# All gate projections ahead of the merge, through DRAM, and a time reserve in the choice of TensorE's next matmul

## The chip, the cores and the metric

The kernel runs as one program on one core of a Trainium2 chip. The metric is the device time of an execution in microseconds (us). The profiled execution is a single one, with its own time; the comparison is made on the median of timed runs.

## What is computed

Two layers of a decoder trunk, over 576 tokens: 512 of a prompt and 64 of eight sampled sequences. One input projection feeds two branches, retention and sparse attention; each branch is gated by a SiLU and projected back to the model's width, and the two are merged by per-channel sigmoid gates:

```python
def decoder_layer(x, p_i, pos, ret_s0, past, topk, ...):
    h = rmsnorm(x, g_norm)
    rq, rk, rv, rz, aq, ak, av, az, iq, ik, iw, gr, ga = in_projection(h, w_in, pos, q_gain, k_gain)
    o_r, s_new = retention(rq, rk, rv, ret_s0)
    o_r = group_norm_heads(o_r).reshape(B, T, RET_HEADS * RET_DV).astype(x.dtype)
    u_r = jnp.einsum('bte,ed->btd', o_r * jax.nn.silu(rz), w_o_ret)
    o_a = sparse_attention(...)          # indexer, top-k, softmax over the chosen keys
    u_a = jnp.einsum('bte,ed->btd', o_a * jax.nn.silu(az), w_o_att)
    m = jax.nn.sigmoid(gr) * u_r + jax.nn.sigmoid(ga) * u_a
    x = x + jnp.einsum('btd,de->bte', m, w_out)
    gate = jax.nn.sigmoid(jnp.einsum('btd,de->bte', x, w_ple_gate))
    x = x + gate * jnp.einsum('btp,pd->btd', p_i, w_ple_proj)
```

The width is 1024, cut into KT = 8 blocks of 128 channels. The gates `gr` and `ga` are 1024 wide each, so each has eight blocks.

## The kernel before

Activations stand transposed, channels on the partitions and tokens along the row: a block is a tile of 128 x 576. Every fp32 operand is split into a high and a low part, and a product takes three matmuls (high x high, high x low, low x high). A **unit** is one weight tile of 128 x 1024: it is loaded by SP's queue into one of two staging buffers (`wst`), split by ACT (`whi`) and DVE (`wlo`), and used by `proj_a` in 48 matmuls of 288 columns (two halves of the tokens, eight blocks, three products). The results of a half stand in one of three PSUM banks named `pm` until DVE or ACT has taken them out.

The order of the instructions is made by a planner in the kernel itself. Each piece of work is a generator that yields operations. `Streams` keeps one modelled clock for each engine and, of all operations that are next in their generators, issues the one with the earliest start; ties go to the lower priority number and then to the older generator. The start is the later of the engine's clock and the time at which the operands are ready. `MARGIN` adds 0.15 us to that ready time for an operation on DVE and 0.1 us for one on ACT, when what it waits for is another engine's work. The result is a fixed order on each engine; the semaphores then make the hardware wait wherever the plan was too early.

The main generator of a layer goes through `PLAN`: the projections of keys (`kx`), indexer (`iq`), values (`rv`), SiLU gate (`az`), attention queries (`aq0`, `aq1`), four retention heads (`rq`, `rk`, `rz` each), then the gates of blocks 0 and 1, and then, for each block d, the output projections `wo` with the merge, followed by the gates of block d + 2. The attention, the indexer's top-k and the retention run as side generators with tiles of their own (`tq`, `ta`, `oT`, `tr`, `acc` are their PSUM banks, one each). The merge begins when all of them have ended (`for e in sides: yield e`). A gate's result is held from its projection to its merge in one of four 576-column slots (`ZS`) cut from the tile `misc`:

```python
                z = yield Get(ZS)
                zt[st] = z
```

The step of the merge multiplies the slot by the output projection, half by half (`mul`), adds the two slots and splits the sum (`fin`), and gives the slots back.

Of the kernel before, what the change touches and what calls it, by code (L numbers as in the profile page):

```python
# [99 lines left out]
    return a, rot  # L100


MARGIN = {"DVE": 0.15, "ACT": 0.1}


class Op:
# [89 lines left out]
class Streams:  # L196
# [15 lines left out]

    def spawn(self, gen, prio):
        self.count += 1
        self.run.append(([gen, prio, self.count, None, 0.0], None))

    def put(self, slots, item):
        if slots.queue:
# [11 lines left out]
    def _advance(self, st, value):  # L230
        gen = st[0]
        while True:
            try:
                x = gen.send(value)
            except StopIteration:
                return
            value = None
            if isinstance(x, Op):
                st[3] = x
                st[4] = self._ready(x)  # L240
                self.heads.append(st)
                return
            if isinstance(x, Get):
                if x.slots.free:
                    value = x.slots.free.pop(0)
                    continue
                x.slots.queue.append(st)
                return
            if x.n > 0:
                x.queue.append(st)  # L250
                return

    def _ready(self, op):
        t = 0.0
        for boxes, w in ((op.ins, False), (op.outs, True)):
            for name, p0, p1, c0, c1 in boxes:
                for e in self.log.get(name, ()):
                    if (w or e[6]) and e[0] < p1 and p0 < e[1] and e[2] < c1 and c0 < e[3]:
                        r = e[4] + self.HOP.get((e[5], op.eng), 0.15)
                        if e[5] != op.eng:  # L260
                            r += MARGIN.get(op.eng, 0.0) 
                        if r > t:
                            t = r
        return t

    def _note(self, op, end):
        low = min(self.clock["PE"], self.clock["DVE"], self.clock["ACT"]) - 5.0
# [11 lines left out]
    def go(self):  # L279
        clock = self.clock  # L280
        while True:
            while self.run:
                st, value = self.run.pop(0)
                self._advance(st, value)
            if not self.heads:
                return
            best = None
            for i, st in enumerate(self.heads):
                key = (max(clock[st[3].eng], st[4]), st[1], st[2])
                if best is None or key < best[0]:  # L290
                    best = (key, i)
            st = self.heads.pop(best[1])
            op = st[3]
            start = best[0][0]
            op.fn(*op.a, **op.k)  # L295
            if op.form != self.form and op.eng == "PE":
                start += 0.09
                self.form = op.form
            end = start + op.dur
            clock[op.eng] = end  # L300
            if op.eng == "SP" and op.name != "page":
                size = _val((op.a[0] if op.a else op.k["out"]).nbytes)
                self.dma = max(self.dma, start + 1.1) + size / 0.35e6
                end = self.dma + 1.0
            self._note(op, end)
            self._advance(st, None)
# [3 lines left out]
def tile_hybrid_decoder(ctx: ExitStack, tc: tile.TileContext, A, O):  # L310
# [46 lines left out]
    cosr, sinr = rot[:, 0:T], rot[:, T:2 * T]  # L357
    ssq = rot[:, 0:TX]
    xd = dp.tile([128, KT, T], FT, name="xd")
    WST = slots(cp, "wst", [128, 1024], FT, 2)  # L360
    WHI = slots(cp, "whi", [128, 1024], FR, NSLOT["hi"])
    WLO = slots(cp, "wlo", [128, 1024], FR, NSLOT["lo"])
# [199 lines left out]
    def layer(l, xh, xl, kxb):  # L562
# [693 lines left out]
        for st in PLAN:  # L1256
            name, i = st[0], st[1:]
            if name == "kx":
                for j in range(5):
                    K.spawn(kx(j, kxb[j]), 0)  # L1260
            elif name == "iq":
                yield from proj_b(U("iq"), 260, 3, xh, xl, (1, 4, 2, 3), iqx)
            elif name == "rv":
                yield from proj_b(U(*st), 256, 4, xh, xl, range(5), rvx(i[0]))
            elif name == "aq":
                yield from proj_b(U(*st), 256, 4, xh, xl, range(5), aqx(i[0]))
            elif name == "az":
                yield from proj_a(U(*st), 0, mv, KT, silu(silz[1][:, i[0]], e_az))
                drop(U(*st))
            elif name in ("rq", "rk", "rz"):  # L1270
                h = i[0]
                t = views(h)
                if name == "rz":
                    ev = silu(silz[0][:, h], e_h[h])
                else:
                    ev = ropeT(t["qT" if name == "rq" else "kT"], e_h[h], e_hd[h - 2] if h > 1 else None)
                yield from proj_a(U(*st), 0, mv, KT, ev)
                drop(U(*st))
                if name == "rz":
                    side(ret_p(h, t), PRIO["ret_p"])  # L1280
                    side(ret_s(h, t), PRIO["ret_s"])
            elif name in ("gr", "ga"):
                if name == "gr" and i[0] == 0:
                    for e in list(e_q.values()) + list(e_iq.values()) + [e_k, e_rr]:
                        yield e
                    ZS = zslots(0, 4)
                z = yield Get(ZS)
                zt[st] = z

                def gate(z):  # L1290
                    def evac(ps, cs):
                        yield V.tensor_tensor(z[:, cs], ps[:, :TH], R[:, cs], OP.mult)
                        K.put(BANK["pm"], ps)
                        yield S.activation(z[:, cs], z[:, cs], AF.Tanh, scale=0.5)

                    return evac

                yield from proj_a(U(*st), 0, mv, KT, gate(z))
                drop(U(*st))
            elif name == "wo":  # L1300
                continue
            elif name == "merge":
                d = i[0]
                if la is None:
                    for e in sides:
                        yield e
                    atc.__exit__(None, None, None)
                    yh = xp.tile([128, KT, TX], FR, name="xh")
                    yl = xp.tile([128, KT, T], FR, name="xl")
                    lac = tc.tile_pool(name="la", bufs=1, reuse_waits="tile")  # L1310
                    la = lac.__enter__()
                    oh = [la.tile([128, 4, T], FR, name=f"oh{x}") for x in range(2)]
                    ol = [la.tile([128, 4, T], FR, name=f"ol{x}") for x in range(2)]
                    e_o = [[Event() for _ in range(4)] for _ in range(2)]
                    for x in range(2):
                        for c in range(4):
                            K.spawn(then(split(oh[x][:, c], ol[x][:, c], silz[x][:, c]), e_o[x][c]), 0)
                    e_m = [Event() for _ in range(KT)]

                th = [zt["gr", d], zt["ga", d]]  # L1320

                def mul(z, ev):
                    def evac(ps, cs):
                        yield V.scalar_tensor_tensor(z[:, cs], z[:, cs], 1.0, ps[:, :TH], op0=OP.add, op1=OP.mult)
                        free(ps)
                        K.set(ev)

                    return evac

                def fin(d, th, ev):  # L1330
                    yield ev
                    yield V.tensor_tensor(th[0], th[0], th[1], OP.add)
                    K.put(ZS, th[1])
                    yield from split(yh[:, d, :T], yl[:, d], th[0])
                    K.put(ZS, th[0])
                    K.set(e_m[d])

                ev = Event(4)
                u = U("wo", d)
                for x in range(2):  # L1340
                    yield from proj_a(u, x * 512, (oh[x], ol[x]), 4, mul(th[x], ev), 0, None if d else e_o[x],
                                      ("oT", "acc") if x and not d else ("pm", "pm"))
                drop(u)
                K.spawn(fin(d, th, ev), 0)
# [159 lines left out]
def _plan(order):  # L1504
    p = []
    for t in order.split():
        n, i = t[:2], t[2:]
        p += [(n,)] if not i else [("rq", int(i)), ("rk", int(i)), ("rz", int(i))] if n == "rt" else [(n, int(i))]
    p += [("gr", 0), ("ga", 0), ("gr", 1), ("ga", 1)]
    for d in range(KT):  # L1510
        p += [("wo", d), ("merge", d)]
        p += [("gr", d + 2), ("ga", d + 2)] if d + 2 < KT else []
    return p + [("wout", d) for d in range(KT)] + [("pp", 0), ("pp", 1)] + [("wpg", d) for d in range(KT)]


# [86 lines left out]
```

## Time and profile before

| | |
|---|---|
| timed runs, median of 3 (lowest to highest) | 1151.29 us (1149.56 to 1151.41) |
| the profiled execution, its own time | 1149.36 us |
| its span, first to last instruction | 1147.4 us |
| mean granted TensorE clock | 0.989 of full speed |
| PE busy | 1099.3 us (96%) |
| DVE busy | 762.7 us (66%) |
| ACT busy | 525.9 us (46%) |
| DMA, mean | 92 GB/s |

All operations are recorded through one helper, so every row bears the line L295; the tiles' names tell the work apart. A matmul's row begins when it starts and lasts until its modelled end, which overlaps the next one: the distance of two starts is the rate. `pm<-xh,whi` is a matmul that writes a `pm` bank from the activations `xh` and the weights `whi`. An "idle before" in brackets is time in which the engine's last row had ended and the next had not begun.

### The profile page before, as it was taken

To read this page: it belongs to the slowest core of one execution; us is meant where nothing else is said; L and a number is where in the kernel's file an instruction comes from. 1 tells how busy PE (TensorE), PEld (TensorE's weight loads), DVE (VectorE), ACT (ScalarE), POOL (GpSimd) and SP (SyncE) were. 2 spreads that over 40 slices of the span, in tenths; PEclk is the share of its full clock that TensorE was granted. 3 is DMA by queue.
4 is the path that set the end of the run, shared out by engine and by line. 5 is a ranking of instruction groups with operands and counts; after the bars stand their busy time and mean duration, and the time that the engine had idled before them with its cause. 6 is when DMAs were issued, how large, how long until landed. Compare 5 with 4: busy or idle time off the path is not lost.

```text
span 1147.4 us, 21421 instructions
## 1 busy us (share of the span) xinstructions
PE 1099.3 (96%) x8426; PEld 1054.0 (92%) x8426; DVE 762.7 (66%) x1979; ACT 525.9 (46%) x1116; POOL 57.9 (5%) x68
## 2 busy tenths in 40 slices
PE   7999799999999999999999996999999999999998
PEld 7889688798899999999998996988899999999998
DVE  6899998667673535543659999886676644454433
ACT  6643455566652222234446434556676422223331
POOL 0100111000000000000010011100000000000000
PEclk9999989999999999999999998999999999999999
DMA  6532121231212222523335212113121222235231
GB/s 193 167 94 82 38 70 60 83 125 54 81 56 93 75 92 74 185 84 113 97 119 163 73 55 75 62 53 130 58 76 62 77 87 81 86 112 158 83 120 47
DMA packets 43894, 105.91 MB, mean 92 GB/s; under 512 B 6418, under 2 KB 18578, under 8 KB 43794
## 3 DMA queue, kind: packets, MB, share of 16 engines
q1 hardware_dynamic: 43794, 104.55, 28.1%
q8 instruction: 66, 1.08, 0.4%
q14 instruction: 34, 0.28, 0.1%
HBM read 93.61 MB, written 10.91 MB: 91 GB/s over the span
## 4 chain that ended last, share of the span: by engine, by line
PE 68%; DVE 23%; ACT 4%; issue 2%; DMA 2%; SPq 0%; POOL 0%; DVEq 0%; ACTq 0%; POOLq 0%
PE pm L295 56%; DVE xl L295 6%; DVE sm L295 5%; DVE wlo L295 3%; PE acc L295 3%; PE tq L295 3%; PE oT L295 3%; DVE misc L295 2%; PE tr L295 2%; PE ta L295 2%; DVE t2k L295 1%; DVE silz L295 1%; DVE qs L295 1%; ACT t2k L295 1%; ACT tb L295 1%
## 5 line engine op out<-in xcount | busy, mean ns | idle before, releaser
L295 PE MATMUL pm<-xh,whi 128*128 128x288 f32 x1536 | 460.0, 299 | 1.0 <-DVE misc L295 1.0
L295 PE MATMUL pm<-xh,wlo 128*128 128x288 f32 x1536 | 458.6, 299 | 0.0
L295 PE MATMUL pm<-xl,whi 128*128 128x288 f32 x1536 | 458.5, 299 | 0.0
L295 PEld LDWEIGHTS pm<-xh,whi 128*128 128x128 f32 x1536 | 292.1, 190 | 2.5 <-DVE misc L295 1.3
L295 PEld LDWEIGHTS pm<-xl,whi 128*128 128x128 f32 x1536 | 292.3, 190 | 1.4 <-issue 0.4
L295 PEld LDWEIGHTS pm<-xh,wlo 128*128 128x128 f32 x1536 | 291.8, 190 | 0.6
L295 ACT ACTIVATE whi<-wst 128x1024 fp32r<-128x1024 f32 (+4 forms) x148 | 150.3, 1017 | 241.2 <-PE pm L295 170.5
L295 DVE TENSOR_TENSOR wlo<-wst,whi 128x1024 fp32r<-128x1024 f32 (+4 forms) x148 | 173.0, 1171 | 85.9 <-ACT whi L295 85.9
L295 PE MATMUL pm<-whi,xh 128*128 128x256 f32 (+2 forms) x416 | 119.5, 293 | 5.5 <-DVE misc L295 2.7
L295 PE MATMUL pm<-wlo,xh 128*128 128x256 f32 (+2 forms) x416 | 119.1, 293 | 0.3 <-DVE wlo L295 0.2
L295 PE MATMUL pm<-whi,xl 128*128 128x256 f32 (+2 forms) x320 | 91.4, 286 | 0.0
L295 PEld LDWEIGHTS pm<-whi,xh 128*128 128x128 f32 x416 | 80.9, 194 | 7.2 <-DVE misc L295 3.4
L295 DVE TENSOR_TENSOR misc<-pm,R 128x288 f32<-128x288 f32 x64 | 29.2, 457 | 83.2 <-PE pm L295 81.7
L295 PEld LDWEIGHTS pm<-wlo,xh 128*128 128x128 f32 x416 | 80.8, 194 | 2.3 <-issue 1.2
L295 ACT ACTIVATE t2k<-t2k,sm 128x256 f32<-128x256 f32 (+3 forms) x111 | 62.5, 578 | 33.2 <-DVE sm L295 30.6
L295 PE MATMUL pm<-oh,whi 128*128 128x288 f32 x240 | 70.9, 296 | 0.0
L295 PE MATMUL pm<-oh,wlo 128*128 128x288 f32 x240 | 70.9, 296 | 0.0
L295 PE MATMUL pm<-ol,whi 128*128 128x288 f32 x240 | 70.9, 295 | 0.0
L295 PEld LDWEIGHTS pm<-whi,xl 128*128 128x128 f32 x320 | 60.5, 189 | 0.1
L295 DVE SCALAR_TENSOR_TENSOR misc<-misc,pm 128x288 f32<-128x288 f32 x60 | 26.8, 452 | 39.3 <-PE pm L295 39.3
L295 DVE MAX8 sm<-xl 128x8 f32<-128x512 f32 (+2 forms) x96 | 52.4, 549 | 0.5
L295 DVE MATCH_REPLACE8 xl<-sm,xl 128x256 f32<-128x256 f32 (+2 forms) x96 | 51.7, 540 | 0.1
(258 smaller groups left out, 1714.5 us busy)
## 6 DMA issues: line engine op xcount, KB each, us to landing
wst<-in_wa SPq DMA_DIRECT2D x96, 512.0 KB, 3.5
wst<-in_wb SPq DMA_DIRECT2D x16, 512.0 KB, 4.0
wst<-in_wo SPq DMA_DIRECT2D x16, 512.0 KB, 3.5
s<-in_ckv SPq DMA_DIRECT2D x32, 128.0 KB, 2.6
s<-in_s SPq DMA_DIRECT2D x8, 512.0 KB, 4.5
out_rss<-s SPq DMA_DIRECT2D x8, 512.0 KB, 2.7
x<-in_xT SPq DMA_DIRECT2D x8, 288.0 KB, 5.9
misc<-in_xT SPq DMA_DIRECT2D x8, 288.0 KB, 3.7
```

Of the source, the lines that this page charges most:

```text
L295: op.fn(*op.a, **op.k)
```

## The change

First, `PLAN` puts all sixteen gate projections of a layer ahead of the merge. Their results can't stay in four slots, so each is written to a DRAM tile (`zd`) when both halves have gone through the tanh, and the slot is given back (`spill`); when the main generator comes to the merge, `fetch` reads the blocks back in order, two slots each, as slots come free.

Second, the planner keeps two times for each operation: the ready time as modelled, and a safe one with the margin. It chooses by the safe one and sets the engine's clock by the modelled one. TensorE gets a margin, 1.0 us. For DVE and ACT the margins stay in the choice and no longer move the clock.

```diff
-MARGIN = {"DVE": 0.15, "ACT": 0.1}
+MARGIN = {"DVE": 0.15, "ACT": 0.1, "PE": 1.0}
...
                         r = e[4] + self.HOP.get((e[5], op.eng), 0.15)
-                        if e[5] != op.eng:
-                            r += MARGIN.get(op.eng, 0.0) 
                         if r > t:
                             t = r
-        return t
+                        if e[5] != op.eng:
+                            r += MARGIN.get(op.eng, 0.0)
+                        if r > safe:
+                            safe = r
+        return t, safe
...
-                key = (max(clock[st[3].eng], st[4]), st[1], st[2])
+                key = (max(clock[st[3].eng], st[5]), st[1], st[2])
...
-            start = best[0][0]
+            start = max(clock[op.eng], st[4])
...
+    zd = {(l, n, d): dp.tile([128, T], FT, name=f"z{n}{l}{d}") for l in range(DEPTH) for n in ("gr", "ga")
+          for d in range(KT)}
...
                 z = yield Get(ZS)
-                zt[st] = z
+                ev = Event(2)
...
+                def spill(z, ev, dst):
+                    yield ev
+                    yield SP.dma_start(dst, z)
+                    K.put(ZS, z)
+
+                K.spawn(spill(z, ev, zd[(l,) + st]), 0)
...
+                    e_g = {k: Event() for k in range(KT)}
+
+                    def fetch():
+                        for k in range(KT):
+                            for n in ("gr", "ga"):
+                                z = yield Get(ZS)
+                                yield SP.dma_start(z, zd[l, n, k])
+                                zt[n, k] = z
+                            K.set(e_g[k])
+
+                    K.spawn(fetch(), 0)
...
+                yield e_g[d]
                 th = [zt["gr", d], zt["ga", d]]
...
-    p += [("gr", 0), ("ga", 0), ("gr", 1), ("ga", 1)]
+    p += [(n, d) for d in range(KT) for n in ("gr", "ga")]
     for d in range(KT):
         p += [("wo", d), ("merge", d)]
-        p += [("gr", d + 2), ("ga", d + 2)] if d + 2 < KT else []
```

The change reorders all engines. Three places show it.

**TensorE, first layer, in the middle of the retention heads and the attention of the second query block.** `acc` and `tr` are banks of the retention, `ta` holds transposed softmax weights, `oT` their product with the values, `pm` a projection. Before:

```order
L295 MATMUL ta_72<-cst,xl 128x128 x2
L295 MATMUL tr_74<-cst,xh 128x128 x2
L295 MATMUL acc_75<-xh 128x128 x2
L295 MATMUL acc_75<-xh,xl 128x128
L295 MATMUL acc_75<-xh 128x128
L295 MATMUL acc_75<-xh,xl 128x128
L295 MATMUL oT_73<-pth_392,vhl 128x256
L295 MATMUL acc_75<-xh 128x128
L295 MATMUL tr_74<-iqs_386,iqs_387 128x512 x2
L295 MATMUL oT_73<-ptl_393,vhl 128x256
```

Now, at the same pair of transposes:

```order
L297 MATMUL ta_72<-cst,xl 128x128 x2
L297 MATMUL acc_75<-xh 128x128
L297 MATMUL ta_72<-cst,t2k_426 128x128 x2
L297 MATMUL pm_68<-xh,whi_123 128x288
L297 MATMUL pm_68<-xl,whi_123 128x288
L297 MATMUL pm_68<-xh,wlo_126 128x288
L297 MATMUL pm_68<-xh,whi_123 128x288
L297 MATMUL pm_68<-xl,whi_123 128x288
L297 MATMUL tr_74<-iqs_418,iqs_419 128x512 x2
L297 MATMUL pm_68<-xh,wlo_126 128x288
L297 MATMUL pm_70<-xh,whi_121 128x288
L297 MATMUL acc_75<-xh 128x128
```

Where side matmuls stood one behind the other, projection matmuls now stand between them.

**VectorE, first layer, where the second set of attention queries (`aq1`) begins.** `MAX` and `MATCH_REPLACE` are rounds of the indexer's top-k on score rows of 384 and 512 columns, `ptl` the low part of the softmax weights, `qs` the low part of the queries. Before:

```order
L295 TENSOR_TENSOR ptl_393<-ta_72,pth_392 128x256
L295 MATCH_REPLACE xl<-sm_384,xl 128x384
L295 MAX sm_382<-xl 128x8
L295 RECIPROCAL sm_380<-sm_380 128x1
L295 MAX sm_383<-xl 128x8
L295 MATCH_REPLACE xl<-sm_382,xl 128x512
L295 MATCH_REPLACE xl<-sm_383,xl 128x384
L295 MAX sm_385<-xl 128x8
```

Now:

```order
L297 TENSOR_TENSOR ptl_425<-ta_72,pth_424 128x256
L297 MAX sm_417<-xl 128x8
L297 MATCH_REPLACE xl<-sm_417,xl 128x384
L297 RECIPROCAL sm_416<-sm_416 128x1
L297 MAX sm_414<-xl 128x8
L297 MATCH_REPLACE xl<-sm_414,xl 128x384
L297 TENSOR_SCALAR xl<-xl 128x384
L297 SCALAR_TENSOR_TENSOR xl<-t2k_428,xl 128x512
```

Two top-k ran side by side here; now the one of 384 columns ends, and the scores of the one of 512 are only being summed.

**SP's queue, first layer, in the merge.** `in_wo` and `in_wa` are weight units, `zgr` and `zga` the gates' DRAM tiles. Before:

```order
L295 DMA wst_87<-in_wo 128x1024
L295 DMA wst_88<-in_wa 128x1024
L295 DMA wst_87<-in_wa 128x1024
L295 DMA wst_88<-in_wo 128x1024
L295 DMA wst_87<-in_wa 128x1024
```

Now:

```order
L297 DMA misc<-zgr_88 128x576
L297 DMA zga_102<-misc 128x576
L297 DMA wst_119<-in_wo 128x1024
L297 DMA misc<-zga_96 128x576
L297 DMA misc<-zgr_89 128x576
L297 DMA wst_120<-in_wo 128x1024
L297 DMA misc<-zga_97 128x576
L297 DMA misc<-zgr_90 128x576
```

Each weight unit of the merge now stands behind two reads of gates.

## Rows read from the trace of the kernel before

**Rows 1.** The page's first part: busy us, share of the span, instructions
```profile
PE 1099.3 (96%) x8426; PEld 1054.0 (92%) x8426; DVE 762.7 (66%) x1979; ACT 525.9 (46%) x1116; POOL 57.9 (5%) x68
```

**Rows 2.** Busy us by stretch: PE, PEld, DVE, ACT, POOL; then clock, DMA share, GB/s
```profile
0.00:50.00 50.00, 41.95 (x295) 40.39 (x295) 35.19 (x111) 34.65 (x81) 5.48 (x10) 1.00 0.55 172
50.00:125.00 75.00, 72.13 (x558) 68.02 (x557) 73.78 (x225) 30.84 (x66) 4.03 (x4) 1.00 0.29 91
125.00:160.00 35.00, 26.45 (x173) 24.41 (x172) 31.98 (x108) 15.02 (x35) 6.12 (x6) 0.85 0.19 59
160.00:330.00 170.00, 164.26 (x1337) 148.85 (x1336) 126.40 (x381) 106.11 (x258) 12.71 (x15) 0.99 0.23 77
330.00:600.00 270.00, 269.94 (x2030) 269.69 (x2029) 133.09 (x206) 98.29 (x166) 3.42 (x5) 1.00 0.32 103
...
675.00:715.00 40.00, 28.73 (x214) 26.72 (x212) 38.73 (x128) 17.72 (x40) 7.76 (x8) 0.94 0.19 56
715.00:910.00 195.00, 188.23 (x1497) 172.07 (x1498) 147.82 (x433) 117.89 (x279) 15.95 (x18) 0.99 0.22 75
```

**Rows 3.** PE's timeline: start, us, engine, operation, idle before; first in the merge
```profile
400.00 0.29 PE L295 MATMUL pm<-xh,wlo 128*128 128x288 f32 x1
400.13 0.29 PE L295 MATMUL pm<-xh,whi 128*128 128x288 f32 x1
...
46.34 0.28 PE L295 MATMUL pm<-whi,xl 128*128 128x256 f32 x1
47.77 0.55 PE L295 MATMUL ta<-cst,misc 128*128 128x128 f32 x3 [1.15 <-ACT misc L295]
```

**Rows 4.** PE's waits, 0 to 50 us: total us, times, longest
```profile
PE ta L295 <- ACT misc L295: 1.2, 1, 1.2
PE tr L295 <- POOL rcol L295: 0.9, 1, 0.9
```

**Rows 5.** PE's waits, 160 to 330 us
```profile
PE tr L295 <- DVE iqs L295: 1.4, 2, 0.8
...
PE tq L295 <- DVE sm L295: 1.0, 1, 1.0
```

**Rows 6.** PE's waits, 715 to 910 us
```profile
PE tr L295 <- DVE iqs L295: 1.9, 2, 1.5
```

**Rows 7.** PE's waits, 125 to 160 us
```profile
PE ta L295 <- DVE qs L295: 4.3, 3, 2.6
```

**Rows 8.** Timeline of all engines at one attention-query tile
```profile
136.53 0.44 PE L295 MATMUL ta<-cst,misc 128*128 128x128 f32 x2 [0.35 <-DVE qs L295]
...
138.34 0.42 DVE L295 TENSOR_TENSOR qs<-ta,qs 64x256 fp32r<-64x256 f32 x1
...
140.50 0.69 PE L295 MATMUL ta<-cst,misc 128*128 128x128 f32 x2 [2.58 <-DVE qs L295]
```

**Rows 9.** The five stretches at half clock, as Rows 2: the first, their sum
```profile
140.00:147.00 7.00, 4.89 (x20) 4.20 (x20) 6.74 (x20) 3.01 (x6) 1.57 (x2) 0.51 0.00 1
...
sum 24.00, PE 20.70 PEld 19.02 DVE 22.27 ACT 7.24 POOL 7.97; mean PE 4.14 PEld 3.80 DVE 4.45 ACT 1.45 POOL 1.59
```

**Rows 10.** DVE's timeline at the end of one merge step
```profile
360.54 0.46 DVE L295 SCALAR_TENSOR_TENSOR misc<-misc,pm 128x288 f32<-128x288 f32 x1 [1.15 <-PE pm L295]
361.02 0.76 DVE L295 TENSOR_TENSOR misc<-misc 128x576 f32<-128x576 f32 x1
```

**Rows 11.** DMA issues: destination, source, count, KB each, median us to landing
```profile
wst<-in_wa SPq DMA_DIRECT2D x96, 512.0 KB, 3.5
...
x<-in_xT SPq DMA_DIRECT2D x8, 288.0 KB, 5.9
...
misc<-xd SPq DMA_DIRECT2D x8, 288.0 KB, 3.0
```

**Rows 12.** SP's timeline: a weight load issued in the merge
```profile
350.06 0.33 SPq L295 DMA_DIRECT2D wst<-in_wo  x1
```

**Rows 13.** ACT's timeline: the conversion of that load
```profile
360.40 1.06 ACT L295 ACTIVATE whi<-wst 128x1024 fp32r<-128x1024 f32 x1 [4.98 <-PE pm L295]
```

More of the change, by code (lines that the diff above doesn't have):

```diff
@@ L214, in spawn @@
         self.count += 1
-        self.run.append(([gen, prio, self.count, None, 0.0], None))
+        self.run.append(([gen, prio, self.count, None, 0.0, 0.0], None))
     def put(self, slots, item):
@@ L239, in _advance @@
                 st[3] = x
-                st[4] = self._ready(x)
+                st[4], st[5] = self._ready(x)
                 self.heads.append(st)
@@ L253, in _ready @@
     def _ready(self, op):
-        t = 0.0
+        t = safe = 0.0
         for boxes, w in ((op.ins, False), (op.outs, True)):
@@ L259, in _ready @@
                         r = e[4] + self.HOP.get((e[5], op.eng), 0.15)
+                        if r > t:
+                            t = r
                         if e[5] != op.eng:
                             r += MARGIN.get(op.eng, 0.0)
-                        if r > t:
-                            t = r
-        return t
+                        if r > safe:
+                            safe = r
+        return t, safe
     def _note(self, op, end):
@@ L1287, in layer, with gate @@
                 z = yield Get(ZS)
-                zt[st] = z
-                def gate(z):
+                ev = Event(2)
+                def gate(z, ev):
                     def evac(ps, cs):
@@ L1294, in evac @@
                         yield S.activation(z[:, cs], z[:, cs], AF.Tanh, scale=0.5)
+                        K.set(ev)
                     return evac
-                yield from proj_a(U(*st), 0, mv, KT, gate(z))
+                def spill(z, ev, dst):
[3 more added lines that the diff above has]
+                K.spawn(spill(z, ev, zd[(l,) + st]), 0)
+                yield from proj_a(U(*st), 0, mv, KT, gate(z, ev))
                 drop(U(*st))
```

## Prediction

> **What bounds the kernel now.** I read the page first, then the busy time by stretch, then TensorE's waits inside the stretches that aren't full, then the timelines at the longest waits. PE is busy for 96% of the span [rows 1], so PE sets the time, and what can be won without taking work away is PE's waiting. The stretches tell where that is [rows 2]. From 330 to 600 us (merge, output and per-layer-input projections of the first layer) PE is busy 269.94 of 270 us at full clock: 288-column matmuls start every 0.13 us [rows 3], and nothing but fewer matmuls would shorten that. All waiting lies where projections are mixed with attention, indexer and retention. There are two kinds of it.
>
> The one kind I call scattered: 2.9 us idle from 50 to 125 us, 5.7 from 160 to 330, 6.8 from 715 to 910 [rows 2], and two waits of 1.2 and 0.9 us before 50 [rows 4]: 17.5 us in 44 waits, nearly all under 1 us, each ended by ACT, DVE or POOL having just finished a softmax, a group norm or the emptying of a bank [rows 4 to 6]. The planner put the matmul there because its model said the operand would be ready; the operand was a little late, and PE takes its matmuls in order.
>
> The other kind is a block in each layer, where the attention queries are projected: 8.6 us idle from 125 to 160, 11.3 from 675 to 715 [rows 2]. Here PE has no projection matmul to do instead: three `pm` banks wait to be emptied, and behind them stands a chain through the one bank `ta`. Two transposes start at 136.53, DVE's first query split at 138.34, the next transposes at 140.50, after a 2.58 us wait [rows 7, 8]. DVE is busy 32.0 of 35 us there and 38.7 of 40 in the second layer [rows 2]. The half clock lies mostly at these blocks, too.
>
> A listed wait understates its cost. At 46.34 a matmul starts and the next, which waits, at 47.77: 1.43 us, where 256 columns take 0.12 and the row lists 1.15 idle [rows 3]. So each wait hides 0.16 us more, because the idle time is counted from the modelled end.
>
> **The reserve.** Without waits PE's work is the same: every matmul is still there, the order of all is changed. What the margin does is visible in the new order. Between two successive score products of the attention (63 pairs, one bank `tq`) the old order has 12 other matmul rows in the median and 6 at least; the new one 17 and 12. Between the transposes of softmax weights and the product that uses them (48 cases) the median goes from 9 rows to 13. At 0.13 us a row [rows 3] that is 0.5 to 0.65 us more work between what PE gives out and what it needs back. It is less than the 1.0 us of the table because the old margins, 0.15 and 0.1 us at each step through DVE and ACT, no longer lengthen the modelled chain. I take 0.6 us.
>
> The scattered waits cost 17.5 + 44 x 0.16 = 24.5 us. Cover of 0.6 us ends all shorter than that and shortens the rest by it; of the nineteen gaps over 0.44 us (among them 1.5, 1.2, 1.0 and 0.9 [rows 4 to 6]) what lies beyond adds up to 5.8 us and remains. So 24.5 - 5.8 = **18.7 us** go. Bounds: nothing, if DVE and ACT simply fall later by the same 0.6 us, and 24.5.
>
> **The gates ahead** supply what stands in front of the side matmuls. In the old order the last attention product of layer 1 has 1561 projection matmuls ahead of it and 47 left before the merge; in the new one 1796, with 388 left. Without the twelve gate units moved forward, the reserve would have run 188 matmuls past the end of the projections, 25 us of PE with little to do. By itself the move wins nothing, because PE did those units at full rate anyway [rows 2].
>
> **The blocks** I leave as they are: the new order has the same 800, 814 to 816, 824 and 840 projection matmuls ahead of each transpose of the second query set, since the banks and not the choice decide there. DVE has less top-k between (the order above), which might shorten the chain; a longer chain is as possible, as the modelled DVE clock has lost its padding. Between 50 and 160 us DVE idles 4.2 us [rows 2]; if it doubled or vanished, the blocks would move by about that much each way. I take 0. But a block limited by DVE gives back part of what is won just before it: PE comes to it earlier and waits for DVE there. Won before it are about 4 us; I take half off, 2 us.
>
> **The transfers** cost PE nothing as I count, and this is what hides them. A write of 288 KB lies between a tanh and the slot's next use, with four slots and one unit of 48 x 0.13 = 6.3 us each. A read in the merge begins when the two slots of a step have been added: the last product of a step starts at 360.54, right as PE ends the step, the add ends at 361.78 [rows 10], 1.5 us after PE's end. Issue 0.33 and landing 3.0 us, as for the same tile read from DRAM [rows 11, 12], make 4.8. It is needed after the next step and a quarter of the one after, 7.9 us, and PE can fill two more `pm` banks, another 3.1. The margin is 6.2 us. If that cover were gone, each of six blocks and two layers would pay what lies beyond. The gates' emptying adds two 0.46 us operations a unit to a DVE that is busy 126 of 170 us [rows 2].
>
> SP gets 64 transfers more, into the one queue of the weights. A spill at the queue's head that waits for its tanh holds back the weights behind it. A load issued at 350.06 lands 3.5 us later and is converted at 360.40 [rows 11 to 13]; so 6.8 us of delay are hidden, more than an emptying takes. The Trainium skill says the same against the change: a DMA's semaphore wait is spent on the issuing sequencer, before the dispatch, and not in the DMA engines (DMA: Bandwidth & Descriptors, in the anatomy of one DMA). By that rule the spill's wait would be charged in full to the next weight load; with the 6.8 us above the sum stays as it is, without them each of 32 spills would show.
>
> **Sum.** Own time of the profiled execution 1149.4; scattered waits -18.7; given back at the blocks +2; transfers 0: 1132.7. The median of the timed runs lies 1.9 us above that execution, so **1134.6 us** as a median, 1.5% less. Its own range goes from 1127 (all scattered waits, nothing given back) to 1142.
>
> **Rivals.**
> *The blocks go, too* (chance 0.15). For it: DVE's order there is thinner, and the blocks are where PE is slowed. Against it: the banks. The five stretches at half clock hold 20.7 us of PE work in 24 us [rows 9], and they stand in or just behind the blocks; half a block's idle time gone, 10 us, and with it half of the 10 us that the clock costs, gives 1134.6 - 15 = about 1120, all of it about 1105. The skill's rule points the same way: the slow clock is the default and activity releases it (TensorE: Matmul & The Clock Gate, Part 1); by it the clock's part follows from the idle part, and the rows agree in that the clock is 1.00 where PE is full [rows 2].
>
> *The reserve is half eaten* (0.17). The side matmuls come later, and the main line waits for them in one place: the query rotation of head h + 2 may not overwrite tiles that retention head h still reads. The old order has head 0's last product after 1119 projection matmuls and head 2's from 1128 on; the new one after 1184, and at 1200 the fourth half needs a bank that this rotation holds: 2.1 us for a chain through DVE and ACT of the kind that cost PE up to 2.6 us in the block [rows 7]. Four such places at 1 to 2 us, or DVE and ACT later by half the cover: some 9 us less gain, 1143.
>
> *Nothing is won* (0.07): the waits move with the plan. 1151.
>
> *Slower* (0.08): the reads come late in the merge. Price: beyond a landing of 3.0 + 6.2 = 9.2 us each of 12 reads delays PE in full; from 10.6 us it outweighs the 16.7 us won; at 12 us it is 34 us, giving about 1169. For it: eight loads of this size at once landed in 5.9 us [rows 11], and the queue carries two reads per weight unit. Against it: the DMA engines are busy 0.32 of the time from 330 to 600 us [rows 2].
>
> **How the numbers follow.** The forecast has 0.53. Differences under 0.2%, 2.3 us, can't be told from none. Faster: 0.53 + 0.15 + 0.17 = 0.85; same 0.07; slower 0.08. For 8 in 10 the range leaves out part of the slower and unchanged cases above and the whole-block case below: 1113 to 1148.
>
> **What would show it.** Right: idle PE from 160 to about 330 and from 715 to about 910 us falls from 12.5 us to 4 or less, while the merge stays full. The blocks keep 7 to 12 us each, at 0.8 to 0.95 clock. The gates' reads land in 3 to 4 us and no merge product waits for one. Wrong: a merge with idle PE, waits of PE on DMA, `pm` waits at the third and fourth head, or side waits of the same number and size as before; and on the other side a block under 4 us.

## The result, and the profile after

The changed kernel takes **1157.35 us** (median of 18 runs, 1152.09 to 1161.79) against 1150.68 us of the kernel before (18 runs, 1149.51 to 1153.2): a ratio of 1.0053, with a 95% interval of 1.0039 to 1.0066. It is half a per cent slower, where 1134.6 us and 1.5% less were forecast, and the time lies outside the range. The profiled execution took 1155.49 us, its span 1153.7; it is compared with the 1149.36 and 1147.4 of before.

The page's first part of after, and below it the busy times by stretch, as in [rows 1, 2] (busy us and instructions of PE, PEld, DVE, ACT, POOL; clock, DMA share, GB/s):

```profile
PE 1098.1 (95%) x8426; PEld 1058.7 (92%) x8426; DVE 764.6 (66%) x1979; ACT 525.7 (46%) x1116; POOL 57.3 (5%) x68
```

```profile
50.00:125.00 75.00, 71.36 (x549) 66.95 (x548) 71.16 (x219) 30.97 (x68) 4.10 (x4) 1.00 0.28 91
125.00:160.00 35.00, 25.85 (x152) 24.01 (x152) 31.20 (x99) 13.64 (x32) 6.15 (x6) 0.76 0.18 60
160.00:330.00 170.00, 160.32 (x1340) 149.72 (x1339) 124.34 (x378) 98.75 (x239) 11.75 (x14) 0.99 0.26 85
330.00:600.00 270.00, 270.00 (x2030) 269.46 (x2029) 138.38 (x215) 106.18 (x183) 3.33 (x5) 1.00 0.40 131
...
715.00:910.00 195.00, 183.53 (x1472) 170.23 (x1473) 140.72 (x424) 108.25 (x258) 15.22 (x18) 0.96 0.26 84
```

The merge is as full as it was, at 270.00 of 270 us, with 131 instead of 103 GB/s moved beside it. The gates' reads land in time: this is the page's list of DMA issues (count, KB each, median us to landing), to be read beside [rows 11].

```profile
zgr<-misc SPq DMA_DIRECT2D x16, 288.0 KB, 2.0
zga<-misc SPq DMA_DIRECT2D x16, 288.0 KB, 2.1
misc<-zgr SPq DMA_DIRECT2D x16, 288.0 KB, 2.8
misc<-zga SPq DMA_DIRECT2D x16, 288.0 KB, 4.6
```

The waiting has not gone. From 160 to 330 us PE idles 9.7 us where it idled 5.7, from 715 to 910 us 11.5 where it idled 6.8. (Part of the second difference is a shift: the block of the second layer ends 4 us later in after. From the end of each block to the merge the idle time is 9.7 and 9.0 us, against 5.7 and 6.5.) These are PE's waits from 160 to 330 us (total us, times, longest), which answer to [rows 5]:

```profile
PE acc L297 <- ACT xh L297: 3.8, 4, 2.2
PE ta L297 <- ACT t2k L297: 3.1, 1, 3.1
PE tr L297 <- DVE iqs L297: 0.9, 1, 0.9
PE tq L297 <- DVE sm L297: 0.9, 2, 0.5
PE oT L297 <- ACT pth L297: 0.7, 1, 0.7
```

Nine waits of 9.4 us in all stand against ten of 5.4 us before, and the long ones are of kinds that were short there:

```profile
PE ta L295 <- ACT t2k L295: 1.1, 3, 0.5
PE acc L295 <- ACT xh L295: 0.4, 1, 0.4
```

The longest wait in this stretch, 3.05 us, shows how one comes about. PE waits for weights of the sampled sequences' attention. On DVE's timeline (start, us, operation, idle before) the first step that those weights need after their maximum is `sm<-sm`, a single column, and the last is `RECIPROCAL`:

```profile
220.71 0.49 DVE L297 TENSOR_REDUCE sm<-tq 128x1 f32<-128x320 f32 x1
221.11 0.29 DVE L297 BATCH_NORM_STATS2 gs<-acc 128x6 f32<-128x128 f32 x1
221.41 0.46 DVE L297 TENSOR_TENSOR xl<-pm,rot 128x288 f32<-128x288 f32 x1
222.78 0.46 DVE L297 TENSOR_TENSOR tb<-tb,rot 128x288 f32<-128x288 f32 x1 [0.90 <-ACT tb L297]
223.15 0.45 DVE L297 TENSOR_TENSOR xl<-pm,rot 128x288 f32<-128x288 f32 x1
223.52 0.45 DVE L297 TENSOR_TENSOR xl<-xl,tb 128x288 f32<-128x288 f32 x1
224.49 0.46 DVE L297 TENSOR_TENSOR tb<-tb,rot 128x288 f32<-128x288 f32 x1 [0.52 <-ACT tb L297]
...
224.91 0.12 DVE L297 TENSOR_SCALAR sm<-sm 128x1 f32<-128x1 f32 x1
...
229.31 0.15 DVE L297 RECIPROCAL sm<-sm 128x1 f32<-128x1 f32 x1
```

The maximum is there at 221.2, its scaling runs at 224.91: between them stand two operations of a rotation that wait 0.90 and 0.52 us for ScalarE. In DVE's fixed order the plan had taken ScalarE's part as done. The same happens a second time on the way: the sum of the exponentials is there at 225.73, its reciprocal runs at 229.31, behind two more waits for ScalarE of 0.41 and 0.64 us and the work between them. From the reduction at 220.71 to PE's row it takes 9.5 us; in the kernel before the first such chain takes 3.2 us, from 213.90 to 217.06. PE's row at the end of the chain, from its timeline:

```profile
230.18 0.55 PE L297 MATMUL ta<-cst,t2k 128*128 128x128 f32 x3 [3.05 <-ACT t2k L297]
```

The time at half clock (a granted share of 0.50) has nearly doubled, from 24.0 us [rows 9] to 44.3. This is the sum row over the six stretches of after:

```profile
sum 44.30, PE 34.28 PEld 30.60 DVE 33.28 ACT 16.37 POOL 9.29; mean PE 5.71 PEld 5.10 DVE 5.55 ACT 2.73 POOL 1.55
```

Two rows of the block of after, in the stretch from 143.5 to 157.2 us, show the rate there: 0.21 us from start to start for 256 columns, where 288 columns take 0.13 at full clock [rows 3].

```profile
145.69 0.41 PE L297 MATMUL pm<-wlo,xh 128*128 128x256 f32 x1
145.90 0.42 PE L297 MATMUL pm<-whi,xh 128*128 128x256 f32 x1
```

So up to half of PE's busy time at half clock is what the clock adds: 17.1 us against 10.35, an estimate of up to 6.8 us more, less where PE would have waited anyway. About half of the added 20.3 us lies outside the attention-query blocks: there the half clock takes 13.6 us, at 273.2 and at 798.9, where it took 3.4 before.

**Blocks and the rest.** For the experiments each span is divided by the work and not by time: a block goes from the start of the 673rd projection matmul (a row that writes `pm`) to the 865th, in the second layer from the 3985th to the 4225th; the order of the projections is the same in all kernels here. Blocks of before, then of after (columns as above):

```profile
124.30:166.50 42.20, 33.65 (x226) 31.35 (x225) 39.18 (x128) 19.85 (x49) 6.12 (x6) 0.88 0.20 63
685.80:735.60 49.80, 40.64 (x282) 38.81 (x281) 45.79 (x148) 26.80 (x63) 8.17 (x8) 0.90 0.18 54
```

```profile
124.20:169.00 44.80, 35.65 (x228) 33.81 (x227) 40.97 (x129) 19.98 (x48) 6.15 (x6) 0.81 0.18 59
687.30:739.70 52.40, 40.88 (x278) 38.38 (x277) 48.62 (x156) 24.64 (x56) 7.48 (x8) 0.87 0.16 51
```

The blocks have grown by 5.2 us together; outside them the span is 1055.4 us before and 1056.5 after. So the forecast gain of 18.7 us did not come at all, and instead of 2 us the blocks took 5.2.

### The profile page after: what moved, and what is told of

It is laid out like the page before. It is cut to its first block, busy times and chain, and to the rows that moved or that the text cites. A ratio compares the mean times of both kernels' runs of the same rounds, so it can differ in the third digit from the quotient of the medians.

```text
span 1153.7 us, 21594 instructions
## 1 busy us (share of the span) xinstructions
PE 1098.1 (95%) x8426; PEld 1058.7 (92%) x8426; DVE 764.6 (66%) x1979; ACT 525.7 (46%) x1116; POOL 57.3 (5%) x68
## 4 chain that ended last, share of the span: by engine, by line
PE 65%; DVE 25%; ACT 4%; issue 3%; DMA 2%; SPq 1%; POOL 0%; DVEq 0%; ACTq 0%
PE pm L297 53%; DVE xl L297 7%; DVE sm L297 5%; DVE wlo L297 3%; PE acc L297 3%; PE oT L297 2%; PE tq L297 2%; PE tr L297 2%; DVE misc L297 2%; PE ta L297 2%; ACT tb L297 1%; DVE silz L297 1%; DVE t2k L297 1%; ACT whi L297 1%; DVE qs L297 1%
## 5 line engine op out<-in xcount | busy, mean ns | idle before, releaser
L297 DVE MAX8 sm<-xl 128x8 f32<-128x256 f32 (+2 forms) x96 | 52.4, 551 | 0.8
L297 DVE MATCH_REPLACE8 xl<-sm,xl 128x384 f32<-128x384 f32 (+2 forms) x96 | 51.8, 541 | 0.0
L297 ACT ACTIVATE misc<-misc 128x288 f32<-128x288 f32 x64 | 27.9, 436 | 44.8 <-DVE misc L297 44.5
```

## The experiments

The kernels were timed beside the kernel before, whose median was 1150.5 to 1150.7 us in each set. The blocks and DVE's busy time in them are given for the first and the second layer, in us. "Outside" is the profiled span less the two blocks. Profiled executions lie up to 4.6 us off their medians (e10's own time is 1133.25, e3's 1153.87), so a difference of 2 us in the last columns decides nothing alone.

| kernel | median us | ratio to before, 95% | blocks | DVE busy in them | outside |
|---|---|---|---|---|---|
| before | 1150.7 | | 42.2, 49.8 | 39.2, 45.8 | 1055.4 |
| after | 1157.4 | 1.0039 to 1.0066 | 44.8, 52.4 | 41.0, 48.6 | 1056.5 |
| e1 gates alone | 1151.6 | 0.9999 to 1.0017 | 43.1, 50.3 | 39.2, 46.0 | 1055.4 |
| e2 planner alone | 1203.6 | 1.0449 to 1.0496 | 45.9, 51.9 | 41.0, 48.6 | 1100.3 |
| e3 margins back | 1150.2 | 0.9985 to 1.0003 | 48.1, 56.1 | 44.0, 52.0 | 1047.9 |
| e4 no reserve | 1164.1 | 1.0102 to 1.0133 | 42.9, 48.9 | 39.0, 44.0 | 1069.8 |
| e5 no reserve in blocks | 1151.5 | 0.9988 to 1.0011 | 45.5, 52.1 | 41.4, 47.6 | 1052.7 |
| e6 reserve within PE's choice | 1148.4 | 0.9968 to 0.9986 | 45.7, 53.7 | 42.9, 50.8 | 1045.7 |
| e7 e1, top-k held | 1143.0 | 0.9921 to 0.9946 | 40.4, 47.5 | 32.2, 39.4 | 1054.4 |
| e8 e3, top-k held | 1142.9 | 0.9911 to 0.9959 | 41.7, 48.9 | 32.1, 39.4 | 1047.8 |
| e9 e1, second bank | 1139.9 | 0.9890 to 0.9921 | 37.0, 45.5 | 34.4, 42.0 | 1055.5 |
| e10 e7, second bank | 1128.7 | 0.9796 to 0.9822 | 31.6, 43.7 | 28.9, 37.5 | 1056.2 |
| e11 e8, second bank | 1133.4 | 0.9844 to 0.9883 | 35.0, 43.1 | 30.1, 38.0 | 1050.6 |
| e12 before, both | 1130.9 | 0.9811 to 0.9845 | 31.6, 43.1 | 28.8, 37.5 | 1053.9 |

### The change taken apart: e1 to e4

e1 takes the planner of before:

```diff
-MARGIN = {"DVE": 0.15, "ACT": 0.1, "PE": 1.0}
+MARGIN = {"DVE": 0.15, "ACT": 0.1}
...
-            start = max(clock[op.eng], st[4])
+            start = best[0][0]
```

> All gates ahead of the merge through DRAM, with the planner of the kernel before (no reserve for TensorE, margins of 0.15 and 0.1 us in the choice and in the clocks of VectorE and ScalarE). Theory A (the margins that left the clocks of VectorE and ScalarE are what costs) and theory B (the reserve itself makes the side chains later) both expect the time of the kernel before, 1150.7 within 2 us: the merge's stretch was full in both traces. Theory C (the gates ahead, with their evictions among the attention's and their 64 transfers, are what costs) expects 1155 to 1158, as the changed kernel's 1157.4, and here the same waits of 2 us and more in the retention part.

e2 is the kernel before with the new planner: the old `PLAN`, the gates in their slots, nothing through DRAM.

> The new planner with the old sequence of projections: gates of blocks d + 2 inside the merge, no DRAM. Theory C expects 1136 to 1143, the gain of 19 us that the reserve was to bring, less what 188 missing matmuls cost. Theories A and B expect no gain: 1155 to 1165, with the slower end if the projections run out before the attention does, which showed as 188 matmuls (25 us) in the order.

e3 changes one line, e4 one number:

```diff
-            start = max(clock[op.eng], st[4])
+            start = max(clock[op.eng], st[4] if op.eng == "PE" else st[5])
```

> The changed kernel with one line different: the clocks of VectorE and ScalarE are again set by the time with the margin, and only TensorE's reserve stays out of its clock. Theory A expects the scattered waits to go here: TensorE's waiting outside the two blocks, 34 us in both traces by start-to-start distances, falls by 10 us or more, and the time is 1138 to 1146. Theory B expects 1155 to 1160, as the changed kernel. Theory C expects no more than 2 us from it.

```diff
-MARGIN = {"DVE": 0.15, "ACT": 0.1, "PE": 1.0}
+MARGIN = {"DVE": 0.15, "ACT": 0.1, "PE": 0.0}
```

> The changed kernel with TensorE's reserve set to 0; the clocks of VectorE and ScalarE stay without margins. Theory A expects it slower than the changed kernel, 1160 to 1170: the modelled chains are too short and nothing covers that. Theory B expects it faster than the changed kernel, 1150 to 1153. Theory C expects about 1157 to 1165.

The gates ahead are free: e1 can't be told from before, and its merge is full as well (PE 269.93 us of 270). Theory C falls. e2 was slower than any theory said. Without the moved gates the projections run out: the last product of the attention comes after all 1608 projection matmuls that a layer has ahead of its merge, in both layers. The row from 320 to 365 us of e2 shows PE with 34.40 of 45 us, at a clock of 0.66:

```profile
320.00:365.00 45.00, 34.40 (x162) 27.21 (x161) 23.36 (x56) 22.64 (x47) 2.46 (x3) 0.66 0.11 37
```

With the gates ahead, e1, e3, e4 and after make a square: the margins in the clocks or not, the reserve or not. The time outside the blocks, us:

| | no reserve | reserve 1.0 us |
|---|---|---|
| margins in the clocks | 1055.4 (e1) | 1047.9 (e3) |
| margins only in the choice | 1069.8 (e4) | 1056.5 (after) |

Taking the margins out of the clocks of DVE and ACT costs 14.4 us without the reserve and 8.6 with it. The reserve wins 13.3 us without the margins and 7.5 with them. The change did both, and they cancel: theory A holds for the rest of the span. The medians of the whole time have the same signs: the margins' loss costs 12.5 and 7.2 us, the reserve wins 6.7 and 1.4 (the last can't be told from none). The reserve's win is also net of the clock. In these profiled executions the half clock outside the blocks takes 3.4 us in e1 and e4, but 10.2 in e3 and 13.6 in after: fewer waits, and longer ones. But e3 was to be 1138 to 1146 and is 1150.16, as fast as before, because its blocks have grown by 10.8 us over e1's. Theory B, which also expected no gain from e3, has e4 faster than after; e4 is 6.7 us slower, so B falls.

### What lengthens the blocks: e3, e5, e6

In the traces of before, after, e1, e3 and e4 a block lasts as long as DVE is busy in it plus 3 to 5 us. That alone doesn't tell which of the two sets the other: a longer block has room for more of DVE's work. What e3 adds is top-k. These are DVE's groups of the first block by line and shape (count | busy us, mean ns), of before and of e3:

```profile
L295 DVE MATCH_REPLACE8 xl<-sm,xl 128x512 f32<-128x512 f32 x7 | 4.7, 673 | 0.0
L295 DVE MAX8 sm<-xl 128x8 f32<-128x512 f32 x6 | 4.1, 684 | 0.0
```

```profile
L297 DVE MAX8 sm<-xl 128x8 f32<-128x512 f32 x10 | 6.8, 680 | 0.1
L297 DVE MATCH_REPLACE8 xl<-sm,xl 128x512 f32<-128x512 f32 x10 | 6.7, 673 | 0.0
```

Seven operations more on 512 columns, 4.7 us. In the second layer's block of e3 the count of both operations is 33 against 23. In after the second block has 30; its first has no more top-k than before (14.1 us against 14.2), but two sums of score rows, 1.5 us, which stood ahead of the block before. These operations can stand in the way: below are a row of PE in e3 and what DVE runs while PE waits.

```profile
140.78 0.55 PE L297 MATMUL pm<-whi,xh 128*128 128x256 f32 x1 [2.08 <-DVE misc L297]
```

```profile
138.01 1.14 DVE L297 MAX8 sm<-xl 128x8 f32<-128x384 f32 x2
139.07 0.07 DVE L297 MATCH_VALUE_LOAD xl<-sm,xl 128x8 f32 x1
139.13 0.54 DVE L297 MATCH_REPLACE8 xl<-sm,xl 128x384 f32<-128x384 f32 x1
139.69 0.42 DVE L297 TENSOR_TENSOR qs<-ta,qs 64x256 fp32r<-64x256 f32 x1
140.15 0.48 DVE L297 SCALAR_TENSOR_TENSOR misc<-pm,rcol,gqk 128x256 f32<-128x256 f32 x1
```

The reserve holds back the indexer's matmuls ahead of the block: in the first layer its last product starts at 92.1 us in before and 91.7 in e1, at 113.0 in e3 and 130.6 in after, and the first top-k operation at 53.2 and 52.7, 63.5 and 61.9. So DVE has less to do ahead of the block: from 50 to 125 us it idles 1.2 us before [rows 2], 3.8 in after, 4.9 in e3. The rounds come later, into the block. e5 and e6 were to tell whether that is what lengthens it. e5 has the planner of e3, with a reserve that the main generator switches off and on:

```diff
...
+                            r += self.reserve if op.eng == "PE" else MARGIN.get(op.eng, 0.0)
...
+            if st == ("aq", 0):
+                K.reserve = 0.0
+            if st == ("rz", 0):
+                K.reserve = MARGIN["PE"]
```

> The kernel of e3 (margins back in the clocks of VectorE and ScalarE, reserve of 1.0 us in TensorE's choice), but the reserve is 0 from the first attention-query projection of a layer until the first head's SiLU gate. In the five traces so far a block (from the 672nd projection matmul to the 864th, and from the 3984th to the 4224th) lasts as long as VectorE is busy in it plus 3.6 to 4.8 us, whatever the planner; in e3 it holds 9 and 15 more top-k rounds and lasts 48.1 and 56.0 us, where e1 has 43.1 and 50.3; outside the blocks e3 is 7.4 us shorter than e1. Theory D (a block is as long as VectorE's work in it, and the reserve postpones top-k rounds into it): the new order leaves a third of the postponed rounds in the blocks, so 45 and 52 us, and 1142 to 1146. Theory E (TensorE's own transposes, chosen 1 us late in the planner's time, lengthen the chain through the one bank): blocks as in e1, 43 and 50, and 1138 to 1141.

e6 has the planner of e3, with another choice:

```diff
-                key = (max(clock[st[3].eng], st[5]), st[1], st[2])
+                key = (max(clock[st[3].eng], st[4 if st[3].eng == "PE" else 5]), st[1], st[2])
...
+            if self.heads[best[1]][3].eng == "PE":
+                best = min(((max(clock["PE"], st[5]), st[1], st[2]), i) for i, st in enumerate(self.heads)
+                           if st[3].eng == "PE")
...
```

> The kernel of e3, but the reserve only decides which matmul TensorE takes: the moment at which TensorE is served among the engines goes by the ready time without it, so what follows a matmul on VectorE isn't queued a microsecond later. Theory D: the top-k rounds in the blocks stay nearly as many as in e3, so do the blocks (47 and 55), and the time is 1147 to 1150. Theory E: the blocks return to 43 and 50 us, and the time is 1138 to 1141.

In e5 the blocks came out at 45.5 and 52.1, the 45 and 52 of theory D, but the time did not, 1151.5 us: most of what they gave was lost outside (1052.7 against 1047.9 in e3). In e6 they are 45.7 and 53.7, between the two theories, with DVE 42.9 and 50.8 busy; theory E's 43 and 50 did not come, and the time, 1148.4, is in theory D's range. It is the only one of e1 to e6 that beats before, by 0.2%. DVE's work in the blocks goes with their length in all of these, but shifting top-k about by the reserve wins little. The next runs take it out.

### Taking the blocks' limits away: e7 to e12

e7 is e1 with this hold, e8 is e3 with it:

```diff
+        blk = [None]
+
-        def topk(x, n, k):
+        def topk(x, n, k, held=False):
             for i in range(0, k, 8):
+                if held and blk[0]:
+                    yield blk[0]
...
-            yield from topk(s, 128, TOPK_P)
+            yield from topk(s, 128, TOPK_P, j > 1)
...
+            if st == ("aq", 0):
+                blk[0] = Event()
+            if st == ("rq", 0):
+                K.set(blk[0])
+                blk[0] = None
```

> The kernel of e1 (no reserve, old planner, gates ahead), with the top-k rounds of the third and fourth query block held while the attention queries are projected; they run later, beside the retention heads. It takes some 9 us of VectorE's work out of each block. Theory D in its strong form: the blocks fall by as much, to 35 and 42 us, the half clock behind them with them, and the time is 1132 to 1138. Rival F (VectorE is busy there because it has time, and the chain through the bank of the transposes sets the length): the blocks fall by 2 us each at most, 1147 to 1150, or 1152 and more if the later top-k makes the attention wait.

> The kernel of e3 with the same hold: both the reserve with padded clocks and the blocks without top-k rounds. Theory D: blocks of 38 and 45 us instead of 48 and 56, the 7 us that e3 wins outside of them kept: 1128 to 1134. Rival F: the blocks fall to those of e1 at best, 43 and 50: 1138 to 1142.

e7 is 0.67% faster than before, but its blocks lose 2.7 and 2.8 us for 7 us of DVE's work: theory D in its strong form falls. Rival F, which allowed the blocks 2 us, is nearer there, and has the time wrong (1147 to 1150 or more, where 1143.0 came). DVE is busy 32.16 of 40.4 us now, and something else sets the length:

```profile
125.10:165.50 40.40, 33.98 (x230) 32.38 (x229) 32.16 (x106) 19.72 (x49) 6.12 (x6) 0.87 0.20 66
```

PE's waits in that block of e7:

```profile
PE ta L297 <- DVE qs L297: 3.8, 3, 1.8
PE pm L297 <- DVE misc L297: 1.6, 2, 1.1
PE tq L297 <- DVE qs L297: 0.9, 1, 0.9
```

The next transposes wait for the one bank to be emptied, as in [rows 7, 8].

e8, at 1142.9 us, is no faster than e7; theory D's 1128 to 1134 did not come, and rival F's 1138 to 1142 nearly. Its blocks, 41.7 and 48.9 us, tell what the postponed top-k does. With the rounds in the blocks the reserve and the padded clocks lengthen them by 5.0 and 5.8 us (e1 to e3); with the rounds held, and DVE's work equal, by 1.3 and 1.4 (e7 to e8). So about three quarters of what the reserve adds to the blocks hangs on top-k. The 6.6 us that e8's profiled execution has less outside than e7's don't show in the medians; why is open.

e9 to e12 give every second tile another bank, one that the retention uses later:

```diff
             def evac(j, ps):
+                bank = "acc" if j % 2 else "ta"
...
-                    b = yield Get(BANK["ta"])
+                    b = yield Get(BANK[bank])
...
```

> The kernel of e1 (gates ahead, old planner, top-k as before) in which the transposes of every second attention-query tile go to the idle bank of the retention sums instead of the one bank that all transposes share. In e1 the blocks last 43.1 and 50.3 us with VectorE busy 38.7 and 46.0; in e7, with 9 us of top-k taken out, 40.4 and 47.6. Theory G (two limits of nearly the same height: VectorE's work, and behind it the chain through the one bank): with the chain widened alone VectorE still sets the length: 40 and 47 us, and 1143 to 1147. Theory F alone (the chain sets it): 36 and 43, and 1134 to 1139. Theory D alone (VectorE): no change, 1150 to 1152.

> e7 (no reserve, top-k held in the blocks) with the second bank of e9: both limits are moved at once. Theory G: the blocks fall below both, to 34 and 44 us, and part of the 24 us at half clock goes with them: 1128 to 1135. Theory F alone: as e9, 36 and 43. If neither bank nor top-k sets the rest (the steps of one tile in a row through VectorE and ScalarE), 40 and 47 stay: 1141 to 1144.

> e10 with the reserve of TensorE and the padded clocks (e8 with the second bank). What the reserve wins outside the blocks, 7 us between e1 and e3 and 6 between e7 and e8, is no longer given back if the blocks were what took it: blocks of 36 and 45 us, and 5 us less than e10: 1124 to 1131. If the reserve pays for itself elsewhere too (top-k and attention crowded against the retention behind the block), no less than e10.

> The kernel before, gates two blocks ahead and nothing in DRAM, with the hold and the second bank of e10. It has twelve units of projections less in front of the merge in each layer. If that cover is needed once the top-k runs later, the last products of the attention run alone before the merge and it is 5 to 15 us slower than e10; if the attention still ends in time (in the kernel before it ends some 50 us of projections ahead), it is as fast as e10, within 2 us.

The bank alone wins 0.95%: blocks of 37.0 and 45.5 us, between theories F and G, and a time, 1139.9, better than G allowed and nearly F's. PE's waits `ta <- DVE qs` in the first block, 4.2 us in e1, are gone in e9 (2.3 us for the last, smaller tile are left, `ta <- DVE qss`). DVE's work in the blocks falls with them, by 4.8 and 4.0 us, though no top-k is held: part of that work was there because the block was long. With both limits moved, as G had it, the first block of e10 is 31.6 us, PE busy 92% of it and at full clock throughout:

```profile
124.10:155.70 31.60, 29.03 (x223) 27.43 (x222) 28.87 (x96) 18.40 (x45) 5.73 (x6) 1.00 0.28 85
675.20:718.90 43.70, 38.58 (x280) 37.36 (x280) 37.46 (x125) 25.52 (x60) 7.84 (x8) 0.92 0.20 62
```

The ratio of **e10**, 0.981, is the best of all. The half clock there is 13.5 us in all, against 24.0 in before and 44.3 in after. The Trainium skill has the rule for such bubbles: the same gap repeating on the engine that should be saturated can mean that there isn't enough SBUF or PSUM for the next tile (Perfetto Trace Analysis, Optimization Strategy). The traces agree: the 2.58 us of [rows 8] was one of three such gaps in the block [rows 7], and one bank more is worth 11.7 us between the medians of e1 and e9.

e11, expected at 1124 to 1131, shows that the reserve still does not pay: 1133.4 against 1128.7, though its profiled execution has 5.6 us less outside the blocks and runs in 1130.4. Its other runs go up to 1138.3 us, at a granted clock of 0.986 to 0.989 where the profiled execution has 0.992; why stays open. e12 has no gates ahead and no DRAM: it lies 2.2 us above e10, its interval overlaps e10's, and the 5 to 15 us of missing cover don't appear. So the twelve units of cover are not needed for this, and the whole gain comes without any part of the change.

## Why the prediction was wrong, point by point

**What bounds the kernel.** Right as to the places: the merge stayed full at 270.00 of 270 us, nearly all waiting lies where projections are mixed with the rest, and there are the two kinds of it.

**The reserve, -18.7 us.** This is the step that failed: the price of the lost margins. The text saw that "the old margins, 0.15 and 0.1 us at each step through DVE and ACT, no longer lengthen the modelled chain", and took 0.4 us off the reserve for that. The square shows the loss of the margins to be worth 14.4 us and the reserve 13.3: net 1.1 us worse outside the blocks. The distance in matmul rows, 12 to 17, is in the order, but it says only how much work stands between two matmuls, not how late what they need will be: in the chain above the operand came 9.5 us after the reduction instead of 3.2. The lower bound in the text, "nothing, if DVE and ACT simply fall later by the same 0.6 us", was the outcome outside the blocks; it had a chance of 0.07. Also with the margins kept the reserve is worth 7.5 us and not 18.7, so its own size was wrong as well; the half clock outside the blocks (10.2 us in e3, 3.4 in e1) took part of it; what took the rest is open.

**The blocks, left as they are with 2 us given back.** Wrong by 3 us in after; in e3 the blocks are 12 us above before. The argument was PE's order: the same number of projection matmuls ahead of each transpose. That is so, but it was DVE's order that changed. The text had the right quantity in hand (DVE idle of 4.2 us between 50 and 160 us, "if it doubled or vanished, the blocks would move by about that much each way") and took 0; it came to 7.6 us, 3.4 more, and the first block grew by 2.6. The half clock that came with the longer idle stretches, up to 6.8 us (part of it inside the blocks' 5.2), had no term on the slow side.

**The transfers, 0, and the gates, 0.** Right: e1 lies at 1.0008. Reads landed after 2.8 and 4.6 us in the median, where 3 to 4 were forecast and 9.2 allowed. The rival on the slow side, with a chance of 0.08, was late reads: it did not occur, and the kernel became slower by another way.

**Gates as cover for the reserve.** Right, as far as it goes: e2 loses 46 us to after. The 188 matmuls and 25 us of the text are those of one layer, so about twice that for both. The make-up differs: in the row above PE isn't only idle, for 10.6 us, but also at a clock of 0.66, which the text left out.

**Blocks go, too (rival).** The price came out about right, for another change: half of the blocks' idle time, with its clock, was put at 15 us. The profiled execution of e10, itself 4.6 us above its median, has 16.7 us less than before in the blocks and 0.8 more outside, and its median is 22 us less; PE's idle time in the blocks falls by 10.0 us, from 17.7 to 7.7. The change does not do it; one bank and a hold of the top-k do.

## What to carry to other kernels

A planner's margin does two things: it spaces the choice, and it slows the modelled clock to the pace of the hardware. Here, moved from the clock to the choice, it had to be priced as lost (14.4 us), and what a reserve on one engine does has to be looked for in the orders of the engines that feed it: count the work that moves into the stretch where they are near their limit. The waits in the blocks shrank (PE's idle time there from 17.7 to 7.7 us in e10) when the resources that they waited for were widened, here by a PSUM bank and by moving some twelve top-k operations a layer out of the block (23 in before, 11 and 12 in e7). The scattered waits are not cured by any of this: outside the blocks e10 has 1056.2 us where before has 1055.4.

## What the runs showed beside that

A short wait is not in the idle time. In the two stretches 170 to 320 and 745 to 900 us before idles 11.1 us and has 2414 matmuls, e3 idles 12.7 us and has 2467; PE is "busy" in both for the time in which one matmul's modelled end covers the late start of the next. The 53 more are not narrower ones: 1362 of those that start there in e3 have 288 columns, against 1159 in before. The rows of matmuls in a stretch, or the distance of their starts, tell more than busy time does, and so does PEld, the second column: 263.7 us before, 274.3 in e3. First before, then e3:

```profile
170.00:320.00 150.00, 144.26 (x1184) 129.20 (x1184) 110.71 (x347) 93.70 (x231) 12.71 (x15) 0.99 0.24 80
745.00:900.00 155.00, 149.63 (x1230) 134.46 (x1229) 111.19 (x330) 95.99 (x233) 11.73 (x14) 1.00 0.23 77
```

```profile
170.00:320.00 150.00, 143.67 (x1218) 134.91 (x1217) 106.44 (x325) 84.68 (x207) 10.61 (x12) 0.99 0.28 92
745.00:900.00 155.00, 148.67 (x1249) 139.36 (x1248) 106.31 (x322) 88.50 (x217) 11.35 (x13) 0.99 0.29 95
```
